# Opening and output projection of a hybrid decoder step: the norm_g spread ahead, masks late on VectorE, banks of their own for the projection, and last stores on two queues

## The chip, the cores and the metric

The kernel runs on one core of a Trainium2 chip. The metric is device microseconds (us) of one execution. The kernel before takes 1124.75 us, the median of 3 runs (1123.86 to 1125.27). Engines are named as in the profile: TensorE is PE (its weight load PEld), VectorE is DVE, ScalarE is ACT, GpSimd is POOL, SyncE is SP.

## What is computed

One decoder layer and a final RMSNorm serve 256 prompt tokens and 64 sample tokens (8 sequences of 8), so 320 tokens of width 2048, all in float32:

```
h = rms_norm(x, norm_g);  p = h @ w_in                    # 2048 -> 12416 columns
y_a = RWKV-7 recurrence of columns of p, times a SiLU gate   # 16 heads of 64
y_b = HGRN2 recurrence of columns of p, times a SiLU gate    # 8 heads of 128
merged = sigmoid(ga) * (y_a @ proj_a) + sigmoid(gb) * (y_b @ proj_b)
y = rms_norm(x + merged @ w_out, final_norm_g)
```

The new states of both recurrences and the last projected row are outputs too.

## The kernel before

Every float32 product is made of three float32r matmuls: both operands are split into a high part (a cast) and a low part (what the cast lost), and hi·hi, lo·hi and hi·lo are summed in one PSUM bank. A block of weights is 1024 rows by 128 columns, 512 KB; ScalarE casts its high part and a second engine subtracts for the low part.

**The opening** (lines 375 to 673) ends with the first tile of the input projection, whose order on TensorE, ScalarE, VectorE and GpSimd is written out by hand. norm_g comes as four rows of 512 (`gq`); ScalarE and VectorE split it into `gr` (lines 574 and 575), four matmuls with selector matrices `sel` spread it over 128 partitions (`gps`, line 578), and VectorE copies it out to `gb` (line 579). Ahead of that VectorE fills the constants `yz`, `qz`, `rs_a`, `rs_b` and others, and behind it `arp`. `warm(n)` issues n matmuls on ones that feed nothing. For each of three token tiles, `squares` and `scale` (ScalarE) find 1/rms, `gain` (VectorE) multiplies by it and by `gb`, `turn` (TensorE) transposes, `high` (ScalarE) and `low` (VectorE) split the transposed tile into `hhi` and `hlo`. `first(part, k4)` is twelve groups of four matmuls of the first projected tile. `half` splits half a weight block, `divide` a whole one, both with GpSimd subtracting (lines 619 and 402). There are three block buffers; `fetch(b, c0, k8)` loads a block into buffer b from SP's queue, and so waits until the block there before it has been split. Loads of small rows (line 420) go through the same queue.

GpSimd also builds masks ahead of `half`: `mk[:, 2]`, two products at line 474, and `mu8`, four casts at line 494 of `mf`.

Next come `rows` and the old shift state, transposed on TensorE and copied by VectorE to `cols` (line 660) and `sst` (line 664).

**The middle** is recorded and put in an order by a planner; every instruction of it carries line 1448. Its order on each engine is fixed ahead of time. It begins with `wd_ad` and `bounds`: VectorE takes `neg` and the first `lbt` difference from `cols`, ScalarE takes an exponential of `lbt`, VectorE goes on with it, and ScalarE and VectorE split the next weight blocks and make `uQ`, `lora_a`, `wst` and `ast`. The first matmul of the middle that needs these is `a<-lora_a,ast`.

**The merge** (lines 1476 to 1494) holds two banks `psf` for `ppa` and `ppb`; its last VectorE reader of a bank is line 1488. **The output projection** (from line 1506) takes six banks from a pool `pso`: three per column block of 512, in two generations, one bank for each token tile. Its matmuls are lines 1531 to 1537, `add` adds the residual and squares on ScalarE. The last column block goes tile by tile, and the third tile (64 rows) in two halves of 256 columns. Each tile then gets its 1/rms (lines 1591 to 1593), four quarter products (lines 1596 to 1600) and two stores from SP's queue (lines 1598 and 1601).

Of the kernel before, what the change touches and what calls it, by code (L numbers as in the profile page):

```python
# [294 lines left out]
def hybrid_step(ctx, tc, x_prompt, x_sample, state_rwkv, state_hgrn, state_shift, norm_g, w_in,  # L295
# [19 lines left out]
    def ctile(shape, name, dt=F32, pool=rconst):  # L315
        return pool.tile(shape, dt, name=name, tag=name)
# [59 lines left out]
    with tc.tile_pool(name="start", bufs=1) as st, \  # L376
# [27 lines left out]

        for k8 in range(2):
            fetch(k8, 128 * 24, k8)

        gr = st.tile([64, 512], F32R, name="gr")
        sel = st.tile([64, 4, 128], F32R, name="sel")
# [13 lines left out]
        for r0, t_ in ((W0, w0), (A0, a0), (KK_, k_k), (KA, k_a), (LW, ln_w), (LB, ln_b), (LG, lb_logits)):  # L423
# [3 lines left out]
        ssr = st.tile([100, 2, 128], F32, name="ssr")  # L427
        nc.sync.dma_start(ssr, state_shift[0].rearrange("s (r c) -> (s r) c", c=128)
                          .rearrange("(j q) c -> q j c", j=2))
        fetch(2, 0, 0)  # L430


        id64 = ctile([128, 64], "id64")
        G.tensor_add(id64, ident[:, 0:64], ident[:, 64:128])
# [37 lines left out]
        blk = seqm[:, :, None].to_broadcast([128, 8, 8])  # L472
        for x in range(2):
            G.tensor_mul(mk[:, 2, x].rearrange("p (s i) -> p s i", i=8),
                         mk[:, 0, x].rearrange("p (s i) -> p s i", i=8), blk)


        mf = st.tile([32, 3, 32], F32, name="mf")
# [2 lines left out]
        for n, sz in enumerate((8, 8, 16)):  # L481
# [8 lines left out]
            G.memset(lv[:, :, 0, :], 0.0)  # L490
            keep_ge(lv[:, :, 1, :], [[-2 * sz, nb], [0, sz]], 0, 1)
            keep_ge(lv[:, :, 1, :], [[2 * sz, nb], [0, sz]], sz - 1, -1)
        for g in range(4):
            G.tensor_copy(mu8[32 * g:32 * g + 32], mf)

        junk = st.tile([128, D], F32, name="junk")
        ssq = [st.tile([128, 2], F32, name=f"ssq{j}") for j in range(3)]

# [40 lines left out]
        def warm(n):  # L539
            for _ in range(n):  # L540
                T.matmul(wps[:, :256], ones[:, :128], ones, start=True, stop=True)

        tps = {}
        with tc.manual_schedule(engines={mybir.EngineType.PE, mybir.EngineType.Activation, mybir.EngineType.DVE,
# [10 lines left out]
                    V.memset(t_[sl, sl].bitcast(F32), x)  # L555
            V.tensor_sub(jr_cent, ident, jr_mean.bitcast(F32))

            yz = ctile([128, 2, 2, 2, 64], "yz")
            yd = ctile([128, 2, 2, 64], "yd")
            qz = ctile([128, NSEQ, 32], "qz")  # L560
# [9 lines left out]
            V.memset(rs_a[:, NP_::8], 0.0)  # L570
            V.memset(rs_b, 1.0)
            V.memset(rs_b[:, ::8], 0.0)

            S.copy(gr[0:4], gq)
            V.tensor_sub(gr[32:36], gq, gr[0:4].bitcast(F32))
            for c_ in range(4):
                ps = pst.tile([128, 512], F32, name="gps", tag="t")
                T.matmul(ps, sel[:, c_], gr, start=True, stop=True)
                V.tensor_copy(gb[:, 512 * c_:512 * c_ + 512], ps)
            V.memset(arp, 0.0)  # L580
            warm(16)
            squares(2)
            scale(2)
            gain(2, 0, 2)
# [70 lines left out]
            first(1, 2)  # L655
            first(2, 2)
            divide(2, 1, G)
            ps = pst.tile([128, 512], F32, name="cps", tag="t")
            T.transpose(ps[:, :128], rows, ident)
            V.tensor_copy(cols, ps[:, :106])  # L660
# [795 lines left out]

    ms = fin.tile([128, KT, 2, NS], F32R, name="ms")

    prj = ExitStack()
    fpr = prj.enter_context(tc.tile_pool(name="fpr", bufs=1))  # L1460
    psf = prj.enter_context(tc.tile_pool(name="psf", bufs=2, space=PSUM))
# [41 lines left out]


    last = ctx.enter_context(tc.tile_pool(name="last", bufs=1))
    pso = ctx.enter_context(tc.tile_pool(name="pso", bufs=2, space=PSUM))
    ssq = last.tile([128, 3, 5], F32, name="ssq")
    rs = [last.tile([128, 1], F32, name=f"rs{j}") for j in range(3)]

# [29 lines left out]
    def add(pt, j, n, c0, w=512):  # L1539
        y = yx[j][:, c0:c0 + w]  # L1540
        if j < 2:
            V.tensor_add(y, y, pt[:, :w])
        else:
            for sl in HS:
                V.tensor_add(y, y, pt[sl, :w])
        jk = last.tile([128, 512], F32, name="jk", tag="jk")
        m = y.shape[0]
        S.activation(jk[:m, :w], y, AF.Square, accum_out=ssq[:m, j, n:n + 1])

    out_tiles = lambda: [pso.tile([128, 512], F32, name=f"po{j}", tag=f"o{j}") for j in range(3)]  # L1550
    tail, coming = [], []
    with tc.manual_schedule(engines={mybir.EngineType.PE}):
        for n in range(3):
            pts = out_tiles()
            for kk in range(8):
                hi, lo = columns(n, kk)
                for q in range(2):
                    for j in range(3):
                        rows(pts[j], j, 2 * kk + q, hi[:, q], lo[:, q])
                step = 8 * n + kk  # L1560
                if step in (1, 2, 3):
                    j = step - 1
                    nc.sync.dma_start(yx[j], x_prompt[0, 128 * j:128 * j + 128, :] if j < 2 else
                                      x_sample.rearrange("b l d -> (b l) d"))
                if step == 4:
                    nc.sync.dma_start(fg, final_g[None, :].to_broadcast([128, D]))
                if step % 2 == 0 and 6 <= step < 20:
                    coming.append(fetch_columns(3, len(coming), last, "t", 2))
                if step % 2 == 1 and 9 <= step < 23:
                    t_ = len(tail)  # L1570
                    tail.append(divide_columns(coming[t_], last, str(t_)))
            for j in range(3):
                add(pts[j], j, n, 512 * n)
                y = yx[j][:, 512 * n:512 * n + 512]
                V.tensor_mul(y, y, fg[:y.shape[0], 512 * n:512 * n + 512])

    with tc.manual_schedule(engines={mybir.EngineType.PE, mybir.EngineType.Activation, mybir.EngineType.DVE}):
        tail.append(columns(3, 7))
        pts = out_tiles()
        for j in range(3):  # L1580

            w = 512 if j < 2 else 256
            for n, pt in enumerate((pts[j],) if j < 2 else (pts[j], pso.tile([128, 512], F32, name="po0", tag="o0"))):
                cs = slice(w * n, w * n + w)
                for k in range(KT):
                    hi, lo = tail[k // 2]
                    rows(pt, j, k, hi[:, k % 2, cs], lo[:, k % 2, cs])
                add(pt, j, 3 + n, 1536 + w * n, w)
            m = yx[j].shape[0]
            r = rs[j][:m]  # L1590
# [4 lines left out]
            y = [yx[j][:, 512 * n:512 * n + 512] for n in range(4)]  # L1595
            V.tensor_scalar(y[0], y[0], r, 0.0, op0=ALU.mult, op1=ALU.add)
            S.activation(y[1], y[1], AF.Copy, scale=r)
            nc.sync.dma_start(dst[:, :1024], yx[j][:, :1024])
            V.scalar_tensor_tensor(y[3], y[3], r, fg[:m, 1536:], op0=ALU.mult, op1=ALU.mult)
            S.activation(y[2], y[2], AF.Copy, scale=r)  # L1600
            nc.sync.dma_start(dst[:, 1024:], yx[j][:, 1024:])


# [26 lines left out]
```

## Time and profile before

| | |
|---|---|
| runs, median of 3 | 1124.75 us |
| the profiled execution | 1124.7 us |
| its span, first to last instruction | 1122.0 us |
| PE busy | 1102.9 us, 98% of the span |
| DVE / ACT / POOL busy | 760.4 / 693.2 / 192.8 us |
| chain that ended last | PE 94%, POOL 2%, ACT 2%, issue 1% |

The profiled execution is 2.7 us longer than its span, which starts with the first instruction. An engine is idle for most of its time without harm where another sets the pace; here TensorE does from about 29 us to 1114 us of the span, and what it waits for there and what lies ahead of it and behind it is what a change can save.

### The profile page before, as it was taken

Reading aid. Unit: us, or ns where it says so; the run is one execution under the profiler, and the core shown is the slowest. Engines: PE = TensorE matmul, PEld = TensorE weight load, DVE = VectorE, ACT = ScalarE, POOL = GpSimd, SP = SyncE. Lnnn points to the kernel's source line nnn. Section 1 sums busy time; section 2 is a strip of 40 time slices with the busy share of each in tenths; the row PEclk is TensorE's granted clock in tenths of the full one; section 3 lists DMA queues with packets and bytes.
Section 4 is the critical chain, followed back from the end, with each engine's and each line's share of the span. In section 5 each row is a group of like instructions: output and inputs, shape, how many; then the busy total and the mean of one; then the engine's idle time right before and its main releaser. Section 6 shows DMA issues by size and latency. Waiting matters only on the chain.

```text
span 1122.0 us, 23659 instructions
## 1 busy us (share of the span) xinstructions
PE 1102.9 (98%) x9240; PEld 1066.5 (95%) x9240; DVE 760.4 (68%) x1618; ACT 693.2 (62%) x1572; POOL 192.8 (17%) x411
## 2 busy tenths in 40 slices
PE   6999999999999999999999999999999999999997
PEld 5999999999999999999999999999999999988886
DVE  8778888887887887887887876444444444437532
ACT  6777777677778678677776876444444444436322
POOL 9531231221311411412312200000000000000000
PEclk9999999999999999999999999999999999999999
DMA  6743545435435436435444354555555555587512
GB/s 177 202 130 107 152 118 146 136 100 157 125 96 158 131 105 165 133 106 159 117 132 137 101 142 142 147 151 150 149 151 150 150 150 149 151 256 267 173 35 93
DMA packets 283107, 159.87 MB, mean 142 GB/s; under 512 B 22893, under 2 KB 273264, under 8 KB 282356
## 3 DMA queue, kind: packets, MB, share of 16 engines
q1 hardware_dynamic: 282996, 158.37, 49.5%
q8 instruction: 72, 1.18, 0.5%
q14 instruction: 39, 0.32, 0.1%
HBM read 148.53 MB, written 9.81 MB: 141 GB/s over the span
## 4 chain that ended last, share of the span: by engine, by line
PE 94%; POOL 2%; ACT 2%; issue 1%; DVE 0%; DMA 0%; ACTq 0%; POOLq 0%; DVEq 0%
PE mps L1448 41%; PE a L1448 10%; PE mps L359 6%; PE mps L360 6%; PE mps L361 6%; PE b L1448 3%; PE po L1531 3%; PE po L1533 3%; PE po L1532 3%; PE ppa L359 2%; PE ppb L360 2%; PE ppb L359 2%; PE ppa L360 2%; PE ppb L361 2%; PE ppa L361 2%; PE y L1448 1%
## 5 line engine op out<-in xcount | busy, mean ns | idle before, releaser
L1448 PE MATMUL mps<-hhi,whi 128*128 128x320 f32 x1088 | 345.1, 317 | 0.0
L1448 PE MATMUL mps<-hlo,whi 128*128 128x320 f32 x1088 | 344.6, 317 | 0.0
L1448 PE MATMUL mps<-hhi,wlo 128*128 128x320 f32 x1088 | 344.1, 316 | 0.0
L1448 PEld LDWEIGHTS mps<-hhi,whi 128*128 128x128 f32 x1088 | 205.0, 188 | 3.6 <-issue 2.7
L1448 PEld LDWEIGHTS mps<-hlo,whi 128*128 128x128 f32 x1088 | 205.1, 188 | 1.1 <-issue 0.4
L1448 PEld LDWEIGHTS mps<-hhi,wlo 128*128 128x128 f32 x1088 | 205.0, 188 | 0.7
L349 ACT CAST whi<-raw 128x1024 fp32r<-128x1024 f32 x88 | 92.4, 1050 | 162.7 <-PE mps L360 107.3
L350 DVE TENSOR_TENSOR wlo<-raw,whi 128x1024 fp32r<-128x1024 f32 x88 | 107.8, 1226 | 124.9 <-ACT whi L349 124.8
L1448 DVE TENSOR_TENSOR wlo<-raw,whi 128x1024 fp32r<-128x1024 f32 x134 | 164.7, 1229 | 17.1 <-ACT whi L1448 15.9
L1448 ACT CAST whi<-raw 128x1024 fp32r<-128x1024 f32 x134 | 140.2, 1046 | 57.0 <-PE mps L1448 54.6
L361 PE MATMUL mps<-hhi,wlo 128*128 128x320 f32 x448 | 138.7, 310 | 0.0
L359 PE MATMUL mps<-hhi,whi 128*128 128x320 f32 x448 | 138.7, 310 | 0.0
L360 PE MATMUL mps<-hlo,whi 128*128 128x320 f32 x448 | 138.7, 309 | 0.0
L361 PEld LDWEIGHTS mps<-hhi,wlo 128*128 128x128 f32 x448 | 84.1, 188 | 0.0
L360 PEld LDWEIGHTS mps<-hlo,whi 128*128 128x128 f32 x448 | 84.1, 188 | 0.0
L359 PEld LDWEIGHTS mps<-hhi,whi 128*128 128x128 f32 x448 | 84.1, 188 | 0.0
L1520 DVE TENSOR_TENSOR wlo<-raw,whi 128x1024 fp32r<-128x1024 f32 x32 | 38.6, 1223 | 39.0 <-ACT whi L1519 38.9
L1519 ACT CAST whi<-raw 128x1024 fp32r<-128x1024 f32 x32 | 33.0, 1050 | 48.5 <-DMA raw<-in_w_out_dram 21.3
L1448 POOL TENSOR_TENSOR vm<-v,seq 96x512 fp32r<-96x512 f32 x16 | 16.9, 1054 | 200.1 <-ACT uK L1448 152.4
L1531 PE MATMUL po<-whi,mhi 128*128 128x512 f32 x128 | 50.1, 392 | 0.7 <-DVE gbt L1488 0.7
L1533 PE MATMUL po<-wlo,mhi 128*128 128x512 f32 x128 | 50.1, 391 | 0.0
L1532 PE MATMUL po<-whi,mlo 128*128 128x512 f32 x128 | 50.0, 391 | 0.0
(435 smaller groups left out, 2244.0 us busy)
## 6 DMA issues: line engine op xcount, KB each, us to landing
raw<-in_w_in_dram SPq DMA_DIRECT2D x194, 512.0 KB
raw<-in_w_out_dram SPq DMA_DIRECT2D x32, 512.0 KB
raw<-in_proj_a_dram SPq DMA_DIRECT2D x16, 512.0 KB
raw<-in_proj_b_dram SPq DMA_DIRECT2D x16, 512.0 KB
s<-in_state_hgrn_dram SPq DMA_DIRECT2D x8, 512.0 KB
out_dram<-s SPq DMA_DIRECT2D x8, 512.0 KB
s<-in_state_rwkv_dram SPq DMA_DIRECT2D x8, 256.0 KB
out_dram<-s SPq DMA_DIRECT2D x8, 256.0 KB
```

Of the source, the lines that this page charges most:

```text
L349: S.copy(hi[:, ks], raw[:, ks])
L350: sub.tensor_sub(lo[:, ks], raw[:, ks], hi[:, ks].bitcast(F32))
L359: T.matmul(dst, hi[:, q, :], xhi[:, k, :], start=(k == 0), stop=False)
L360: T.matmul(dst, hi[:, q, :], xlo[:, k, :], start=False, stop=False)
L361: T.matmul(dst, lo[:, q, :], xhi[:, k, :], start=False, stop=(k == nk - 1))
L1448: o.fn(*o.args, **o.kw)
L1519: S.copy(hi, raw)
L1520: V.tensor_sub(lo, raw, hi.bitcast(F32))
L1531: T.matmul(pt, h, hi, start=first, stop=False)
L1532: T.matmul(pt, l, hi, start=False, stop=False)
L1533: T.matmul(pt, h, lo, start=False, stop=end)
```

## The change

- The split and spreading of norm_g moves ahead of the constants; its four copies out of PSUM alternate between ScalarE and VectorE; `warm(16)` becomes `warm(20)`.
- The load of the third weight block is issued ahead of the small rows.
- The products for `mk[:, 2]` and the casts for `mu8` move from GpSimd to VectorE, behind the split of the third block.
- The output projection takes its first generation of banks from a pool opened ahead of `psf` (`pso[0]`), the second behind it (`pso[1]`).
- At the end, the squares carry the factor 1/D, the sum of the earlier partial squares and the epsilon are made ahead of the last `add`, and the logarithm takes that sum as its bias and the last partial as its input. The third tile's columns 1536 to 1791 get final_norm_g during the last matmuls. The products are cut anew, and the store of columns 1024 to 2047 goes first, from SP's queue, that of columns 0 to 1023 second, from ScalarE's queue.

```diff
+        fetch(2, 0, 0)                                   # ahead of the rows, line 404
...
-        fetch(2, 0, 0)                                   # behind ssr, line 430
...
-        for x in range(2):
-            G.tensor_mul(mk[:, 2, x]..., mk[:, 0, x]..., blk)
...
-        for g in range(4):
-            G.tensor_copy(mu8[32 * g:32 * g + 32], mf)
...
             V.tensor_sub(jr_cent, ident, jr_mean.bitcast(F32))
+            S.copy(gr[0:4], gq)
+            V.tensor_sub(gr[32:36], gq, gr[0:4].bitcast(F32))
+            for c_ in range(4):
+                ps = pst.tile([128, 512], F32, name="gps", tag="t")
+                T.matmul(ps, sel[:, c_], gr, start=True, stop=True)
+                (V.tensor_copy if c_ % 2 else S.copy)(gb[:, 512 * c_:512 * c_ + 512], ps)
             ... (constants)
-            S.copy(gr[0:4], gq)
-            ... (the same with V.tensor_copy alone)
             V.memset(arp, 0.0)
-            warm(16)
+            warm(20)
...
             divide(2, 1, G)
+            for x in range(2):
+                V.tensor_mul(mk[:, 2, x]..., mk[:, 0, x]..., blk)
+            for g in range(4):
+                V.tensor_copy(mu8[32 * g:32 * g + 32], mf)
             ps = pst.tile([128, 512], F32, name="cps", tag="t")
...
+    pso = [ctx.enter_context(tc.tile_pool(name="pso0", bufs=1, space=PSUM))]
     prj = ExitStack()
...
-    pso = ctx.enter_context(tc.tile_pool(name="pso", bufs=2, space=PSUM))
+    pso.append(ctx.enter_context(tc.tile_pool(name="pso1", bufs=1, space=PSUM)))
...
-        S.activation(jk[:m, :w], y, AF.Square, accum_out=ssq[:m, j, n:n + 1])
+        S.activation(jk[:m, :w], y, AF.Square, scale=D ** -0.5, accum_out=ssq[:m, j, n:n + 1])
...
+                if 512 == w * (n + 1):
+                    V.tensor_reduce(r, ssq[:m, j, :3 + n], axis=mybir.AxisListType.X, op=ALU.add)
+                    V.tensor_add(r, r, eps_n[:m])
                 add(pt, j, 3 + n, 1536 + w * n, w)
+                if j == 2 and n == 0:
+                    y = yx[j][:, 1536:c1]
+                    V.tensor_mul(y, y, fg[:m, 1536:c1])
-            V.tensor_reduce(r, ssq[:m, j, :4 + j // 2], axis=mybir.AxisListType.X, op=ALU.add)
-            S.activation(r, r, AF.Ln, scale=1.0 / D, bias=eps_n[:m])
+            S.activation(r, ssq[:m, j, 2 + 512 // w:3 + 512 // w], AF.Ln, bias=r)
             S.activation(r, r, AF.Exp, scale=-0.5)
+            V.scalar_tensor_tensor(y[:, c1:], y[:, c1:], r, fg[:m, c1:], op0=ALU.mult, op1=ALU.mult)
+            S.activation(y[:, 0:512], y[:, 0:512], AF.Copy, scale=r)
+            V.tensor_scalar(y[:, 1024:c1], y[:, 1024:c1], r, 0.0, op0=ALU.mult, op1=ALU.add)
+            nc.sync.dma_start(dst[:, 1024:], y[:, 1024:])
+            S.activation(y[:, 512:768], y[:, 512:768], AF.Copy, scale=r)
+            V.tensor_scalar(y[:, 768:1024], y[:, 768:1024], r, 0.0, op0=ALU.mult, op1=ALU.add)
+            nc.scalar.dma_start(dst[:, :1024], y[:, :1024])
```

Here c1 is 1536 for the first two tiles and 1792 for the third.

## Rows read from the trace of the kernel before

**Rows 1.** TensorE's waits over the span: total us, times, longest us.
```profile
PE gps L578 <- DVE gr L575: 6.8, 1, 6.8
PE a L1448 <- DVE ast L1448: 0.9, 1, 0.9
...
PE po L1531 <- DVE gbt L1488: 0.7, 1, 0.7
PE mps L612 <- POOL wlo L619: 0.4, 1, 0.4
```

**Rows 2.** Chain that ended last, 0 to 60 us: start, us, what.
```profile
28.56 4.51 DMA raw<-in_w_in_dram
...
33.17 1.05 ACT whi L1448
...
38.12 0.53 PE a L1448 x2
```

**Rows 3.** Timeline of the opening, until 12.5 us: start, us, engine, line, operation, count.
```profile
3.26 0.48 DVE L563 MEMSET yz<- 128x512 f32 x1
...
5.93 0.68 DVE L575 TENSOR_TENSOR gr<-gq,gr 4x512 fp32r<-4x512 f32 x1
6.64 1.91 ACT L502 ACTIVATE junk<-xt 64x2048 f32<-64x2048 f32 x1 [3.54 <-DMA xt<-in_x_sample_dram]
...
6.76 2.04 PE L578 MATMUL gps<-gr,sel 64*128 64x512 f32 x4 [6.76 <-DVE gr L575]
...
7.56 2.49 DVE L579 COPY gb<-gps 128x512 f32<-128x512 f32 x4 [0.95 <-PE gps L578]
...
8.73 3.78 PE L541 MATMUL wps<-ones 128*128 128x256 f32 x16
...
10.26 1.12 DVE L580 MEMSET arp<- 128x1280 f32 x1 [0.21 <-issue]
...
11.30 6.19 DVE L513 SCALAR_TENSOR_TENSOR xt<-xt,ssq,gb 64x1024 f32<-64x1024 f32 x6
```

**Rows 4.** The same timeline, GpSimd alone, until 29 us.
```profile
10.02 6.27 POOL L474 TENSOR_TENSOR mk<-mk,seqm 128x64 f32<-128x64 f32 x2
...
21.14 5.04 POOL L619 TENSOR_TENSOR wlo<-raw,whi 128x512 fp32r<-128x512 f32 x4
...
26.12 2.41 POOL L402 TENSOR_TENSOR wlo<-raw,whi 128x1024 fp32r<-128x1024 f32 x1
```

**Rows 5.** The same timeline, ScalarE and VectorE, 24 to 31 us.
```profile
24.77 1.06 ACT L401 CAST whi<-raw 128x1024 fp32r<-128x1024 f32 x1
...
27.29 0.27 DVE L660 COPY cols<-cps 128x106 f32<-128x106 f32 x1 [1.57 <-PE cps L659]
...
27.75 0.82 DVE L1448 TENSOR_SCALAR neg<-cols 128x16 f32<-128x16 f32 x1
...
30.53 0.21 ACT L1448 ACTIVATE lbt<-lbt 128x8 f32<-128x8 f32 x1
```

**Rows 6.** Timeline of the end, from 1115 us.
```profile
1115.49 0.15 DVE L1591 TENSOR_REDUCE rs<-ssq 64x1 f32<-64x5 f32 x1 [0.64 <-ACT jk L1548]
1115.67 0.29 ACT L1592 ACTIVATE rs<-rs,eps_n 64x1 f32<-64x1 f32 x1 [0.22 <-DVE rs L1591]
...
1116.24 0.48 DVE L1596 TENSOR_SCALAR xb<-xb,rs 64x512 f32<-64x512 f32 x1 [0.60 <-ACT rs L1593]
1116.64 0.74 DVE L1599 SCALAR_TENSOR_TENSOR xb<-xb,rs 64x512 f32<-64x512 f32 x1
...
1116.98 0.49 SPq L1598 DMA_DIRECT2D out_dram<-xb  x1
1117.60 0.51 SPq L1601 DMA_DIRECT2D out_dram<-xb  x1
```

**Rows 7.** Busy time by stretch: us, engines (count), granted clock, DMA share, GB/s.
```profile
1110.00:1112.80 2.80, 2.80 (x26) 2.80 (x25) 0.83 (x2) 0.51 (x2) 0.00 (x0) 1.00 0.94 375
1118.10:1120.80 2.70, 0.00 (x0) 0.00 (x0) 0.00 (x0) 0.00 (x0) 0.00 (x0) 0.60 0.92 194
```

More of the change, by code (lines that the diff above doesn't have):

```diff
@@ L471, in hybrid_step @@
                 keep_ge(mk[sl, c_], [[1, 2], [1, 64]], -1, -1)
-        blk = seqm[:, :, None].to_broadcast([128, 8, 8])
-        for x in range(2):
-            G.tensor_mul(mk[:, 2, x].rearrange("p (s i) -> p s i", i=8),
-                         mk[:, 0, x].rearrange("p (s i) -> p s i", i=8), blk)
         mf = st.tile([32, 3, 32], F32, name="mf")
@@ L572, in hybrid_step @@
             V.memset(rs_b[:, ::8], 0.0)
-            S.copy(gr[0:4], gq)
[L575 to L579, printed above, removed]
             V.memset(arp, 0.0)
-            warm(16)
+            warm(20)
             squares(2)
@@ L657, in hybrid_step @@
             divide(2, 1, G)
+            blk = seqm[:, :, None].to_broadcast([128, 8, 8])
+            for x in range(2):
+                V.tensor_mul(mk[:, 2, x].rearrange("p (s i) -> p s i", i=8),
+                             mk[:, 0, x].rearrange("p (s i) -> p s i", i=8), blk)
+            for g in range(4):
+                V.tensor_copy(mu8[32 * g:32 * g + 32], mf)
             ps = pst.tile([128, 512], F32, name="cps", tag="t")
@@ L1547, in add @@
         m = y.shape[0]
-        S.activation(jk[:m, :w], y, AF.Square, accum_out=ssq[:m, j, n:n + 1])
-    out_tiles = lambda: [pso.tile([128, 512], F32, name=f"po{j}", tag=f"o{j}") for j in range(3)]
+        S.activation(jk[:m, :w], y, AF.Square, scale=D ** -0.5, accum_out=ssq[:m, j, n:n + 1])
+    out_tiles = lambda n: [pso[n % 2].tile([128, 512], F32, name=f"po{j}", tag=f"o{j}") for j in range(3)]
     tail, coming = [], []
@@ L1553, in hybrid_step @@
         for n in range(3):
-            pts = out_tiles()
+            pts = out_tiles(n)
             for kk in range(8):
@@ L1578, in hybrid_step @@
         tail.append(columns(3, 7))
-        pts = out_tiles()
+        pts = out_tiles(3)
         for j in range(3):
             w = 512 if j < 2 else 256
-            for n, pt in enumerate((pts[j],) if j < 2 else (pts[j], pso.tile([128, 512], F32, name="po0", tag="o0"))):
+            m = yx[j].shape[0]
+            r = rs[j][:m]
+            c1 = D - w
+            for n, pt in enumerate((pts[j],) if j < 2 else (pts[j], pso[0].tile([128, 512], F32, name="po0", tag="o0"))):
                 cs = slice(w * n, w * n + w)
@@ L1587, in hybrid_step @@
                     rows(pt, j, k, hi[:, k % 2, cs], lo[:, k % 2, cs])
+                if 512 == w * (n + 1):
+                    V.tensor_reduce(r, ssq[:m, j, :3 + n], axis=mybir.AxisListType.X, op=ALU.add)
+                    V.tensor_add(r, r, eps_n[:m])
                 add(pt, j, 3 + n, 1536 + w * n, w)
-            m = yx[j].shape[0]
-            r = rs[j][:m]
-            V.tensor_reduce(r, ssq[:m, j, :4 + j // 2], axis=mybir.AxisListType.X, op=ALU.add)
-            S.activation(r, r, AF.Ln, scale=1.0 / D, bias=eps_n[:m])
+                if j == 2 and n == 0:
+                    y = yx[j][:, 1536:c1]
+                    V.tensor_mul(y, y, fg[:m, 1536:c1])
+            S.activation(r, ssq[:m, j, 2 + 512 // w:3 + 512 // w], AF.Ln, bias=r)
             S.activation(r, r, AF.Exp, scale=-0.5)
             dst = y_prompt[0, 128 * j:128 * j + 128, :] if j < 2 else y_sample.rearrange("b l d -> (b l) d")
[L1595 to L1601, printed above, removed]
+            y = yx[j]
+            V.scalar_tensor_tensor(y[:, c1:], y[:, c1:], r, fg[:m, c1:], op0=ALU.mult, op1=ALU.mult)
[5 more added lines that the diff above has]
+            nc.scalar.dma_start(dst[:, :1024], y[:, :1024])
 _INS = ['x_prompt', 'x_sample', 'state_rwkv', 'state_hgrn', 'state_shift', 'norm_g', 'w_in',
```

## The prediction

> **What bounds the kernel.** I read the chain that ended last first: 94% of it is TensorE, so only the ends of the span and TensorE's waits can give time. TensorE's waits come next [rows 1]: the first matmul stands 6.8 us until norm_g is split, then 0.4 us for GpSimd's low weights, 0.9 us for `ast`, and 0.7 us at the first matmul of the output projection. Then the chain of the opening [rows 2]: the load that ends at 33.07 holds ScalarE's cast at 33.17, and that leads to the matmul `a` at 38.12. Last the timelines of the opening, engine by engine [rows 3 to 5], and of the end [rows 6]. The reader should see that VectorE is late with norm_g for no reason but its place in line, and that GpSimd begins on the weights only at 21.14 because masks lie ahead of them.
>
> **The spread of norm_g.** VectorE could take the subtraction at 3.26 instead of 5.93 [rows 3]. The first of the four matmuls began 0.83 us behind it (6.76 against 5.93) and they took 2.04, so they run from 4.09 to 6.13. VectorE needed 2.49 for four copies; its two now end about 0.7 behind the last matmul, at 6.8, and ScalarE's two about 6.3, inside the 3.54 us in which ScalarE waits for the samples until 6.64. The constants then take what they took, 2.67 (3.26 to 5.93), and `arp` 1.04 (10.26 to 11.30): the gains begin at 6.8 + 3.7 = 10.5 instead of 11.30, 0.8 us earlier. Most of the possible 2.7 us stays with VectorE, since the constants only change places with norm_g. Four more warm matmuls at 3.78/16 = 0.24 are 0.95 us: they end at 6.06 + 4.7 = 10.8, while the first transpose must wait for the first gain, about 1.2 us from 10.5. They cost nothing; without that cover they would cost at most 0.95.
>
> **The load ahead of the small rows.** The block's cast at 24.77 had no wait before it [rows 5], so nothing is gained there. The rows move behind one more 512 KB load; a load behind a full queue took about 4.5 us [rows 2], which puts their landing near 20 us, ahead of `cols` at 27. Cost 0; without that slack at most those 4.5 us.
>
> **The masks leave GpSimd.** The two products at 10.02 took 6.27 us [rows 4]. Without them and the casts GpSimd can start on the weights when ScalarE's first cast is there, near 17 instead of 21.14, so TensorE's 0.4 us wait goes. By then TensorE is 0.8 + 0.4 = 1.2 us ahead. ScalarE follows TensorE there, so the cast of the third block ends at 25.83 - 1.2 = 24.65, GpSimd subtracts from 24.65 to 27.05 instead of 26.12 to 28.53, and the load behind it lands 1.5 us earlier. Since both TensorE's head start and this load are 1.2 to 1.5 us ahead and 0.9 us of waiting at `a` lies between, the opening could give 1.5 to 2.0 us.
>
> **The masks arrive on VectorE.** They are two products of 64 columns and four casts of 96; by `cols`, 0.27 us for 106 columns [rows 5], I take 0.2 us each, 1.2 in all. VectorE waited 1.57 us ahead of `cols`, which seems to hide them. But rows of both engines show that each can hold the other up. `neg`, 16 columns, took 0.82 us and ended at 28.57, just when GpSimd's subtraction ended at 28.53 [rows 4, 5]. And the two mask products took GpSimd 6.27 us while the gains ran. In the changed kernel the gains of the second half meet GpSimd's first subtractions (5.04/4 = 1.26 us each, from about 17 on), which delays VectorE by up to 0.9 us. So the first mask product becomes ready about when, or just after, the long subtraction starts at 24.65, and waits until 27.05. Two products until 27.45; then GpSimd's next subtraction, whose block now is there in time, until 29.85; beside it the casts and `cols`; then `neg`, and the `lbt` difference, some 0.35 us; ScalarE's exponential of `lbt` at 30.2 instead of 30.53 [rows 5]. Everything behind it on ScalarE (two weight casts, `uQ`, `lora_a`, `ast`) keeps its distance, so `a` comes at 37.8 instead of 38.12. TensorE, there 1.2 us earlier, waits 1.75 us instead of 0.85. The opening gives 0.3 us. The bounds: 2.0 us gained if the two engines never meet, and 0.9 us lost if GpSimd does both subtractions in a row (24.65 to 29.45) before VectorE gets one product: then 1.2 for the masks, 0.46 for `cols` and `sst`, 0.35 for `neg` and `lbt` put the exponential at 31.45. I take 0.3 gained, between them, because `neg` shows one instruction's wait and not two.
>
> The Trainium skill has the rule for it ("SBUF — State Buffer", section "Who interferes with whom"): a VectorE instruction with two SBUF inputs, or in a two-port mode, and a GpSimd instruction that reads SBUF shut each other out, and "issue order, not op shape, decides who blocks". The 0.82 us of `neg` agrees. By it the opening gives about 1.8 us if the product is issued before the subtraction and 0.3 if behind it; which of them comes first is too close for the rows to tell.
>
> **The banks.** TensorE's 0.7 us at the first matmul of the output projection ends when VectorE has read the last bank of the merge (line 1488) [rows 1]. With the first generation in other banks that reason is gone; the next thing it needs, the first weights and the first merged rows, is long there, since ScalarE and VectorE work one to three blocks ahead. I take the whole 0.7 us; the bounds are 0, if another wait replaces it, and 0.7.
>
> **The end.** The logarithm can begin where the reduction began, 1115.49 instead of 1115.67 [rows 6]: 0.18 us. Then VectorE has the 256-column product (0.74 for 512, so about 0.45) and the 768-column one (0.48 for 512, about 0.6): from 1116.06 they end near 1117.1, and the first store goes out at 1117.1 instead of 1116.98. The second goes out near 1117.4 instead of 1117.60. The two stores of 64 rows moved 194 GB/s between them from 1118.10 to 1120.80, while those of 128 rows reached 375 [rows 7]: with 64 rows it is the transfer that is slow, and the second store had no gap to lose. So what counts is when the first goes out: 0.1 us lost. If the two queues ran side by side at full rate, the second's own time would count, about 0.9 us gained; if ScalarE's queue, which carries no store before, is slower to start than SP's, up to 0.6 lost.
>
> The Trainium skill speaks against the second queue ("DMA: Bandwidth & Descriptors", section "Issuing engines are not separate DMA queues"): transfers started by different engines run on the same 16 DMA engines and interleave. By it this part is the 0.1 us lost; no run here shows it yet.
>
> **The sum.** -0.3 - 0.7 + 0.1 = -0.9 us on the profiled execution's 1124.7: 1123.8 us. The median of the runs is 0.05 higher, which changes nothing.
>
> **The rivals.**
> - *VectorE gets its products in first.* For it: VectorE's 1.57 us of room. Against it: `neg`. Opening -1.8, sum -1.8 - 0.7 + 0.1 = -2.4: 1122.3 us; with stores side by side as well 1121.4.
> - *GpSimd does both subtractions first.* For it: the second now needs no load that is late. Opening +0.9, sum +0.3: 1125.0 us.
> - *TensorE's clock falls at `a`* (slower). In the case before, TensorE would arrive at 36.1 and wait until 39.0, about 3 us. The granted clock of 0.60 from 1118.10 to 1120.80 [rows 7], with only 1.0 and 0.5 to mix, puts its fall at about 1118.6, 4.7 us after the last matmul; the 0.9 us waits cost none. If a wait of some 4 us at `a` brings the level of 1.2 GHz for 4 us, half of these are lost, 2 us: sum +2.3, 1127.0 us. [...]
> - *The banks don't help*, since another wait stands at the same place: sum -0.2, 1124.5 us.
>
> **Chances and range.** Forecast 0.44, VectorE first 0.28, GpSimd first 0.16, banks 0.06, clock 0.06. About 0.2% (2.25 us) is what can be told from no change. The first rival lies on that line or beyond, so faster gets 0.27; slower by as much needs the clock or a slow queue on top of a loss, 0.06; the same 0.67. The range runs from 1121.6, nearly all of the first rival, to 1125.6, past the second; the forecast's own is 1123.2 to 1124.4.
>
> **What would show it.** In the new profile: gains from about 10.5; no wait for GpSimd's low weights; the first mask product on VectorE far longer than 0.2 us, ending with a GpSimd subtraction; ScalarE's `lbt` exponential near 30.2, and a wait at `a` of more than 0.9 us. No wait at line 1531's first matmul. The last store issued near 1117.4 less what the front gave, and the stores' rate still near 200 GB/s. If `lbt` comes before 29, the two engines did not meet and the prediction is too slow; if gains don't start before 11, its first step is wrong.

## The result and the profile after

Before: 1124.36 us (median of 22 runs, 1123.65 to 1125.27). After: 1126.03 us (22 runs, 1124.15 to 1128.46); ratio 1.0013 [1.0007, 1.0018]. The change makes the kernel slightly slower. The profiled execution took 1126.66 us with a span of 1124.9, against 1124.7 and 1122.0. The spans differ by 2.9 us, the times by 2.0: what lies around the span was 2.7 us in the run profiled before and 1.76 in this one, and it is about 1.7 in most runs of both. So the working below goes by the spans. It is the working of one execution, and one of the longer ones: the 22 spans of the changed kernel reach from 1122.4 to 1126.7 us, with a median of 1124.0.

TensorE runs the same list of matmuls in both kernels, so the first question is how late one and the same matmul starts in each. The table gives its start less its start before, worked out from the two traces (+ is later); the rows below the second are the experiments.

| kernel (start before, us) | first of block 0 (18.22) | `cols` transpose (26.98) | `a` (38.12) | 57.26 | 988.34 | 1025.77, output projection | last (1113.67) |
|---|---|---|---|---|---|---|---|
| after | +1.36 | +0.68 | +2.30 | +3.69 | +3.72 | +2.81 | +2.81 |
| e1 masks back | +1.53 | +0.84 | -0.01 | -0.01 | -0.08 | -0.99 | -0.99 |
| e2 spread back | -0.13 | +0.02 | +1.33 | +2.90 | +2.93 | +2.02 | +2.02 |
| e3 warm 28 | -0.28 | -0.15 | +1.17 | +2.74 | +2.72 | +1.81 | +1.81 |
| e4 banks and end | -0.09 | +0.23 | -0.14 | -0.15 | -0.14 | -1.05 | -0.49 |
| e5 e1, warm 28 | -0.24 | -0.26 | -0.77 | -0.76 | -0.79 | -1.70 | -0.95 |
| e6 products early | +1.62 | +0.93 | +2.19 | +3.74 | +3.74 | +3.11 | +3.21 |
| e7 gains first | -1.37 | -2.05 | -2.56 | -2.57 | -2.57 | -3.47 | -3.47 |
| e8 one queue | +0.92 | +0.61 | -0.34 | -0.35 | -0.31 | -1.21 | -1.21 |
| e9 casts on ScalarE | +1.97 | +1.30 | +0.44 | +0.44 | +0.39 | -0.52 | -0.52 |
| e10 products last | -1.38 | -1.92 | -1.92 | -1.92 | -1.97 | -2.88 | -2.88 |
| e11 last block on VectorE | -1.35 | -1.86 | -2.36 | -2.36 | -2.33 | -3.24 | -3.24 |

All of the loss is made by 44 us, and nothing is added in the 940 us after it. The banks give 0.91 back at one place. Then 1124.9 - 2.81 = 1122.1 against 1122.0: the end costs 0.1.

TensorE's waits of after (total us, times, longest), which answer to [rows 1]:

```profile
PE gps L554 <- DVE gr L551: 4.4, 1, 4.4
PE a L1446 <- DVE ast L1446: 2.5, 1, 2.5
PE tps L517 <- DVE xt L505: 2.0, 1, 2.0
```

The waits for GpSimd's weights and for the bank at the output projection are gone. In their place the wait at `a` grew from 0.9 to 2.5 us, and one of 2.0 us stands ahead of the first transpose. In the kernel before, that transpose follows the warm matmuls (done at 12.51) without a wait; its own wait for a gain, 0.8 us, came only at 16.89:

```profile
12.51 0.79 PE L525 MATMUL tps<-ident,xt 64*128 64x64 f32 x8
```

The timeline of the opening, answering to [rows 3]:

```profile
3.24 1.05 DVE L551 TENSOR_TENSOR gr<-gq,gr 4x512 fp32r<-4x512 f32 x1
4.44 2.04 PE L554 MATMUL gps<-gr,sel 64*128 64x512 f32 x4 [4.44 <-DVE gr L551]
6.42 3.94 PE L533 MATMUL wps<-ones 128*128 128x256 f32 x20
6.52 0.69 DVE L555 COPY gb<-gps 128x512 f32<-128x512 f32 x1 [0.16 <-PE gps L554]
7.27 0.48 DVE L562 MEMSET yz<- 128x512 f32 x1
...
10.11 1.12 DVE L572 MEMSET arp<- 128x1280 f32 x1 [0.19 <-issue]
11.15 6.06 DVE L505 SCALAR_TENSOR_TENSOR xt<-xt,ssq,gb 64x1024 f32<-64x1024 f32 x6
12.36 0.85 PE L517 MATMUL tps<-ident,xt 64*128 64x64 f32 x8 [2.01 <-DVE xt L505]
```

The warm matmuls moved 2.3 us ahead with norm_g, the gains only 0.15. The twenty took 3.94 us, and not the 4.7 that the spacing of before would make: they started 0.21 us apart until 9.36 and 0.12 apart from there on, where the trace's record of the granted clock begins, at 1.00. In the kernel before it begins at 12.74, and all sixteen stood at the wider spacing. So TensorE, done at 10.35, stood idle for 2.01 us. The windows of after show what followed, there and behind the wait at `a`. A line gives the length of the stretch, the busy time (and count) of PE, PEld, DVE, ACT and POOL, the granted clock (1.00 or 0.50), the DMA share and GB/s:

```profile
9.40:12.70 3.30, 1.29 (x13) 1.09 (x13) 3.00 (x5) 3.22 (x5) 3.19 (x3) 1.00 1.09 342
12.80:19.50 6.70, 6.70 (x36) 6.09 (x34) 5.71 (x7) 3.60 (x9) 6.23 (x10) 0.50 0.67 163
19.70:40.00 20.30, 17.57 (x123) 17.04 (x122) 18.64 (x33) 13.95 (x31) 13.18 (x20) 1.00 0.57 151
40.10:43.40 3.30, 2.98 (x11) 3.01 (x12) 2.33 (x6) 2.41 (x5) 2.63 (x9) 0.50 1.20 290
```

The same two stretches that stand at 0.50 here, in the kernel before:

```profile
12.80:19.50 6.70, 5.84 (x47) 4.62 (x45) 6.70 (x9) 4.75 (x11) 6.55 (x14) 1.00 0.59 158
40.10:43.40 3.30, 3.30 (x26) 3.30 (x25) 2.38 (x5) 2.97 (x9) 1.83 (x8) 1.00 0.56 137
```

TensorE ran at 1.2 GHz instead of 2.4 in both: 36 matmuls instead of 47, and 11 instead of 26. The second stretch is the step from +2.30 to +3.69 in the table, 1.39 us. What made `a` late is in the timeline of 26 to 41 us, answering to [rows 4, 5]:

```profile
26.59 4.79 POOL L402 TENSOR_TENSOR wlo<-raw,whi 128x1024 fp32r<-128x1024 f32 x2 [1.23 <-ACT whi L401]
26.71 4.75 DVE L652 TENSOR_TENSOR mk<-mk,seqm 128x64 f32<-128x64 f32 x2
31.38 0.84 DVE L655 CAST mu<-mf 32x96 uint8<-32x96 f32 x4
32.25 0.27 DVE L658 COPY cols<-cps 128x106 f32<-128x106 f32 x1
32.37 0.38 ACT L1446 COPY pad<-mps 128x256 f32<-128x256 f32 x1 [3.55 <-issue]
32.71 0.17 DVE L1446 TENSOR_SCALAR neg<-cols 128x16 f32<-128x16 f32 x1
32.98 0.21 ACT L1446 ACTIVATE lbt<-lbt 128x8 f32<-128x8 f32 x1 [0.23 <-DVE lbt L1446]
...
40.42 0.60 PE L1446 MATMUL a<-lora_a,ast 128*128 128x320 f32 x1 [2.46 <-DVE ast L1446]
```

Two products of 64 columns took VectorE 4.75 us, just as long as GpSimd's two subtractions of 1024 beside them. `cols` is 5 us later than in [rows 5], ScalarE's exponential of `lbt` 2.45, and `a` 2.30. The late VectorE reached ScalarE in two ways. ScalarE stood idle for 3.55 us ahead of `pad`, the first of its instructions in the middle, and went on 0.15 us behind VectorE's last cast, which ended at 32.22; SP's next load was issued at 32.36. The profile names no reason for that wait; it fits memory of the opening that is free only when `mf` has been read. The wait for `lbt` itself added 0.23 us.

The end of after, answering to [rows 6, 7]:

```profile
1118.87 0.48 DVE L1603 SCALAR_TENSOR_TENSOR xb<-xb,rs 64x256 f32<-64x256 f32 x1 [1.20 <-ACT rs L1600]
1119.27 0.61 DVE L1605 TENSOR_SCALAR xb<-xb,rs 64x768 f32<-64x768 f32 x1
1119.90 0.49 SPq L1606 DMA_DIRECT2D out_dram<-xb  x1
1120.22 0.54 ACTq L1609 DMA_DIRECT2D out_dram<-xb  x1
```

And the window in which these two stores move:

```profile
1120.80:1123.00 2.20, 0.00 (x0) 0.00 (x0) 0.00 (x0) 0.00 (x0) 0.00 (x0) 0.50 0.92 194
```

Less the 2.81 us by which all of it is late, the first store goes out 0.11 later than before, the second 0.19 earlier, and the rate is the same 194 GB/s.

### The profile page after: what moved, and what is told of

Read it like the earlier page. It is cut to its first block, busy times and chain, and to the rows that moved or that the text cites. A ratio compares the mean times of both kernels' runs of the same rounds, so it can differ in the third digit from the quotient of the medians.

```text
span 1124.9 us, 23677 instructions
## 1 busy us (share of the span) xinstructions
PE 1106.3 (98%) x9244; PEld 1070.6 (95%) x9244; DVE 766.5 (68%) x1629; ACT 694.1 (62%) x1574; POOL 190.3 (17%) x405
## 4 chain that ended last, share of the span: by engine, by line
PE 96%; ACT 2%; DVE 1%; issue 1%; POOL 0%; DVEq 0%; ACTq 0%; POOLq 0%
PE mps L1446 42%; PE a L1446 10%; PE mps L361 6%; PE mps L359 6%; PE mps L360 6%; PE b L1446 3%; PE po L1533 3%; PE po L1531 3%; PE po L1532 3%; PE ppb L361 2%; PE ppb L359 2%; PE ppa L361 2%; PE ppa L359 2%; PE ppb L360 2%; PE ppa L360 2%; PE y L1446 1%
```

## The experiments

**The theory** was that two parts of the change lose time, each in its own way: the masks hold VectorE behind GpSimd's subtractions, which makes `a` late and drops the clock behind its wait; and the spread leaves TensorE idle ahead of the first transpose, which drops the clock there. **Rivals**: one of the two is the cause of everything, or late memory or loads are. The median of the kernel before lies between 1123.9 and 1124.0 us beside these runs, and the ratios are taken against its runs.

**e1, masks back on GpSimd**, all else of the change kept.

```diff
+            G.tensor_mul(mk[:, 2, x].rearrange("p (s i) -> p s i", i=8),
...
+            G.tensor_copy(mu8[32 * g:32 * g + 32], mf)
...
             divide(2, 1, G)
-                V.tensor_mul(mk[:, 2, x].rearrange("p (s i) -> p s i", i=8),
...
-                V.tensor_copy(mu8[32 * g:32 * g + 32], mf)
```

> The changed kernel with the masks back on GpSimd, where the kernel before has them. Theory: the masks on VectorE carry the loss at `a`. Then VectorE's `cols` comes back from 32.25 to about 27.3 to 28, ScalarE's `lbt` exponential to 30 to 31, `a` from 40.42 to about 38.1, and the granted clock does not fall at 40. The fall at 12.77 stays, since TensorE still idles from its last warm matmul to the first transpose, but the wait at `a` takes up what it costs: opening about 0, banks and end -0.8, so about 1123.6 us against 1124.4. Rival: the slow TensorE of 12.77 to 19.60 is what makes everything late; then `a` stays above 39.5 and the time near 1125.5 to 1126.

Measured: 1122.65 us, ratio 0.9987 [0.9979, 0.9996]; the span is 0.8 us shorter than before, as expected, and the median 1.3. `cols` at 28.13, the exponential at 30.40, `a` at 38.11 without any wait. The matmul `a` and two windows of it:

```profile
38.11 0.39 PE L1446 MATMUL a<-lora_a,ast 128*128 128x320 f32 x1
12.60:19.30 6.70, 6.70 (x38) 6.24 (x37) 5.93 (x7) 3.15 (x8) 6.51 (x14) 0.50 0.64 156
40.10:43.40 3.30, 3.30 (x26) 3.30 (x24) 2.12 (x3) 3.10 (x8) 2.09 (x9) 1.00 0.61 151
```

The clock still falls at the first transpose, and not at `a`. So without the masks the loss is gone: 3.7 us by the two traces, 2.9 by the medians, each against the kernel before. The loads stand here as in the change, so they are not its cause. Without the masks the change is faster than the kernel before.

**e2, norm_g spread where it was**, with 16 warm matmuls; masks on VectorE.

```diff
-            S.copy(gr[0:4], gq)
...
-                (V.tensor_copy if c_ % 2 else S.copy)(gb[:, 512 * c_:512 * c_ + 512], ps)
...
             V.memset(rs_b[:, ::8], 0.0)
+            S.copy(gr[0:4], gq)
...
+                V.tensor_copy(gb[:, 512 * c_:512 * c_ + 512], ps)
             V.memset(arp, 0.0)
-            warm(20)
+            warm(16)
```

> The changed kernel with norm_g spread where the kernel before has it (16 warm matmuls); masks still on VectorE. Theory: the gap ahead of the first transpose falls back to 0.8 us, so the clock does not fall at 12.77; the masks still hold VectorE until a GpSimd subtraction ends, twice, so `cols` comes near 31 to 32 and `a` near 39.5 to 40.4, the wait at `a` is 2.5 to 3.2 us and the clock falls there again: +2.5 to +3.7 in the opening, -0.8 behind it, 1126 to 1127 us. Rival: the products were late only because the slow TensorE shifted them against the subtractions; then `cols` comes by 29, `a` by 38.1, and the time is 1123.6 or less.

Measured: 1127.09 us, 1.0026 [1.0016, 1.0036], 0.1 above what was expected; the profiled run, 1125.87, is the shortest of its nine. TensorE's wait at `a` is 2.2 us, 0.3 below the expected range. VectorE's products, and then two windows:

```profile
26.79 3.71 DVE L651 TENSOR_TENSOR mk<-mk,seqm 128x64 f32<-128x64 f32 x2
```

```profile
12.80:19.50 6.70, 5.95 (x47) 4.71 (x45) 6.70 (x9) 4.85 (x12) 6.70 (x11) 1.00 0.65 157
40.40:43.60 3.20, 3.20 (x15) 3.16 (x14) 1.95 (x4) 3.01 (x7) 2.93 (x13) 0.50 0.87 208
```

No fall at the first transpose, but the masks wait all the same and the clock falls behind `a`: the second fall needs no first. What the first one costs the changed kernel is less clear. In the traces e2 is 0.8 us ahead of the change, but by the medians it is slower (1127.09 against 1126.03, and 1124.3 against 1124.0 by the spans), so a loss by the early spread is not shown in the usual execution.

**e3, 28 warm matmuls instead of 20**, all else as in the change.

```diff
-            warm(20)
+            warm(28)
```

> The changed kernel with 28 warm matmuls in place of 20, so that TensorE has work until about 12.3 us, when the first gain ends. Theory: the idle 2.0 us before the first transpose are what let the clock fall at 12.77; bridged, the clock stays at 2.4 GHz there, transposes run at the spacing of before and the first matmul of part 0 begins near 18.2 instead of 19.57. The masks still hold VectorE, so `a` stays near 40 with a wait of 3 us or more and the fall at 40: time about that of the changed kernel, 1125.5 to 1126.5 us. Rival: the first fall is what made the masks late as well; then `a` comes by 38.5 and the time is 1123.6 to 1124.4. Second rival: the fall at 12.77 has another cause and comes again.

Measured: 1125.61 us, 1.0009 [1.0000, 1.0018]. The 28 were done at 11.34 and not at 12.3, since they too ran 0.12 us apart from 9.4 on; but the wait ahead of the first transpose is 1.0 us instead of 2.0, and the fall is gone (a clock of 1.00 in the first window). `a` still waits 2.2 us:

```profile
12.36 0.71 PE L517 MATMUL tps<-ident,xt 64*128 64x64 f32 x8 [1.02 <-DVE xt L505]
12.80:19.50 6.70, 5.64 (x44) 4.39 (x42) 6.70 (x9) 5.34 (x12) 6.70 (x9) 1.00 0.67 161
40.20:43.50 3.30, 3.30 (x15) 3.26 (x14) 1.98 (x4) 3.10 (x8) 2.95 (x13) 0.50 0.83 199
```

Only the warm matmuls, and with them the idle time, were changed, so idleness in the opening was the cause of the first fall. Of the eleven runs, five have spans of 1122.3 to 1122.4 and six of 1123.9 to 1124.9. A gap of 1.5 us is what the fall behind `a` costs here (+1.17 to +2.74 in the table), so it may come in some executions only; just one run has a trace, so this is argued and not shown. The runs of the change itself fit: in six the mean granted clock is 0.996 or 0.997, with spans of 1122.4 to 1123.4, and in sixteen, the profiled one among them, 0.993 or 0.994, with 1123.6 to 1126.7.

**e4, banks and end alone**, opening of the kernel before.

```diff
+    pso = [ctx.enter_context(tc.tile_pool(name="pso0", bufs=1, space=PSUM))]
...
+    pso.append(ctx.enter_context(tc.tile_pool(name="pso1", bufs=1, space=PSUM)))
...
+            nc.scalar.dma_start(dst[:, :1024], y[:, :1024])
```

> The kernel before with only the banks and the end of the change; its opening untouched. Theory: all of the loss is made before 44 us; between 44 and 996 us the changed kernel's TensorE stands 3.69 to 3.73 us late without a step, then the banks give back 0.91, and the last stores land 0.12 later against TensorE's end. So -0.9 + 0.1 = -0.8 us: 1123.6 us against 1124.4. Rival: the end costs or gives more than the one profile shows (two queues that start the stores apart), from -1.8 to 0.

Measured: 1123.14 us, 0.9991 [0.9982, 1.0000], the -0.8 that was expected. In its profiled run the banks give 0.91 as well, and 0.56 is lost again between 1032 and 1040 us, where TensorE waits 0.3 us for VectorE's low weights; e5 loses 0.75 in the same place, e6 0.1, the others nothing. What sets that stays open.

**e5, e1 with 28 warm matmuls.**

```diff
-            warm(20)
+            warm(28)
```

> The changed kernel with the masks back on GpSimd and 28 warm matmuls. With 20 the clock still fell at 12.52, TensorE ran 0.84 us late to `cols`, and yet `a` came at 38.11, without a wait. Theory: the fall at the first transpose costs nothing there, since `a` follows ScalarE's and VectorE's chain to `ast`. Bridged, the clock stays up, TensorE is some 1 us earlier, waits that long at `a`, and `a` comes at 37.7 to 38.2; time within 0.4 us of 1122.65. Rival: the chain to `ast` follows TensorE (through the transposes that ScalarE and VectorE read), and `a` comes 0.8 us or more earlier: 1121.8 us or less.

Measured: 1122.72 us, 0.9987 [0.9978, 0.9996]: the time is that of e1. Its trace speaks for the rival: `a` comes 0.76 us earlier than in e1, so the chain to `ast` does follow TensorE; what was won is lost in the output projection, as told at e4. But e8 below has the opening of e1, with the same fall, and its `a` is only 0.43 us behind that of e5. So the first fall is worth 0.4 to 0.8 us at `a` where nothing else holds `a`, and nothing that shows in the time.

**e6, the two products ahead of the gains on VectorE**, the casts of `mu8` left late.

```diff
             V.memset(arp, 0.0)
+            blk = seqm[:, :, None].to_broadcast([128, 8, 8])
+            for x in range(2):
+                V.tensor_mul(mk[:, 2, x].rearrange("p (s i) -> p s i", i=8),
...
             warm(20)
...
             divide(2, 1, G)
-            blk = seqm[:, :, None].to_broadcast([128, 8, 8])
-            for x in range(2):
-                V.tensor_mul(mk[:, 2, x].rearrange("p (s i) -> p s i", i=8),
...
```

> The changed kernel with the two mask products on VectorE moved ahead of the gains, right behind the memset of `arp`; the four casts of `mu8` stay late on VectorE. Theory: not the work but its place beside GpSimd's long subtractions cost the time. Near 11.2 GpSimd runs only short instructions, so the products take 0.2 us each (at most 0.5), the gains begin near 11.6, the casts take 0.84 us in all near 26.7, `cols` comes near 27.6, `lbt` by 31, `a` near 38.1 to 38.5, and the clock does not fall at 40: 1122.7 to 1123.4 us. Rival: the six instructions cost VectorE their time wherever they stand, or the casts' release of the opening's memory alone makes `a` late; then `a` is past 39.3 and the time 1125 or more.

Measured: 1125.53 us, 1.0012 [1.0003, 1.0021]. This expectation failed:

```profile
11.15 0.30 DVE L575 TENSOR_TENSOR mk<-mk,seqm 128x64 f32<-128x64 f32 x2
...
26.84 4.78 POOL L402 TENSOR_TENSOR wlo<-raw,whi 128x1024 fp32r<-128x1024 f32 x2 [1.23 <-ACT whi L401]
26.98 5.13 DVE L655 CAST mu<-mf 32x96 uint8<-32x96 f32 x4
32.15 0.27 DVE L658 COPY cols<-cps 128x106 f32<-128x106 f32 x1
```

Early, both products take 0.30 us. But now the first two casts stand where the products stood and take 2.33 and 2.36 us, one GpSimd subtraction each; the last two take 0.20 each. The theory missed that a cast from SBUF waits like a product. What remained open was whether this, or the late reading of `mf`, which keeps the opening's memory, makes `a` late.

**e9, e6 with the casts on ScalarE.**

```diff
             divide(2, 1, G)
-            for g in range(4):
-                V.tensor_copy(mu8[32 * g:32 * g + 32], mf)
...
+            for g in range(4):
+                S.copy(mu8[32 * g:32 * g + 32], mf)
             for j in range(4):
                 S.copy(seq4[32 * j:32 * j + 32], seqm[0:32, 0:4])
```

> The run with the products ahead of the gains, and with the four casts of `mu8` on ScalarE, ahead of its copies of `seq4`; nothing of the masks is left on VectorE behind GpSimd's long subtractions. In the run before it the first cast took 2.33 us and the second 2.36, each until a GpSimd subtraction ended (29.25, 31.62), and the other two 0.20 each. Theory: this lock carries the loss, and not that `mf` is read late, which keeps the opening's memory. Then `cols` comes near 27.9, the four casts cost ScalarE 0.8 us (near 27.6 to 28.4) that it has idle, `a` comes at 38.0 to 38.6, the clock does not fall at 40, and the time is 1122.6 to 1123.4 us. Rival: the late reader of `mf` is what holds ScalarE, SP and GpSimd; it still reads at 28.4, some 2.5 us later than without, and `a` stays past 39.3, the time 1124.5 or more.

Measured: 1122.74 us, 0.9988 [0.9979, 0.9997]. The casts, still late, cost ScalarE 1.11 us, and VectorE is free:

```profile
27.96 1.11 ACT L667 CAST mu<-mf 32x96 uint8<-32x96 f32 x4
28.59 0.27 DVE L656 COPY cols<-cps 128x106 f32<-128x106 f32 x1 [1.18 <-PE cps L655]
30.60 0.37 ACT L1446 COPY pad<-mps 128x256 f32<-128x256 f32 x1
```

`a` comes at 38.57 without a wait, and the clock does not fall there; at the first transpose it does, behind a wait of 2.4 us. So the loss comes from VectorE's waits behind GpSimd, and reading `mf` until 29.07 costs nothing. But its memory is not cleared as a link: in after `mf` is read until 32.22 and in e6 until 32.11, and in both `pad` began some 0.15 us later. Whether VectorE's late casts held ScalarE by the memory or by `lbt`, which came 0.2 us behind, no run tells apart. The four casts may even be late, if not on VectorE.

**e8, both stores of e1 from SP's queue.**

```diff
-            nc.scalar.dma_start(dst[:, :1024], y[:, :1024])
+            nc.sync.dma_start(dst[:, :1024], y[:, :1024])
```

> The changed kernel with the masks back on GpSimd, and with both stores of a row block issued by SP. Theory: the two queues give nothing by themselves, since the two stores share the rate of the first run (194 GB/s between them): the last landing stands within 0.15 us of where it stands with two queues, measured from TensorE's last matmul, and the time is that of the run with two queues, 1122.65, to 0.3 us. Rival: SP issues the second store 0.5 us or more later, behind the first one's issue, and the end is as much longer.

Measured: 1122.85 us, 0.9986 [0.9977, 0.9995]. From the last matmul's place, the span ends at 1120.9 + 1.21 = 1122.1, and in e1 at 1121.2 + 0.99 = 1122.2: one queue or two makes no difference, though SP issues the second store at 1116.47, 0.59 behind the first, and ScalarE in e1 0.32 behind.

**e7, gains first**: e1 with `rs_b` behind the second gain and `arp` in the late place where the masks had been.

```diff
-            V.memset(rs_b, 1.0)
-            V.memset(rs_b[:, ::8], 0.0)
-            V.memset(arp, 0.0)
             warm(20)
...
             gain(2, 2, 2)
+            V.memset(rs_b, 1.0)
+            V.memset(rs_b[:, ::8], 0.0)
...
             divide(2, 1, G)
+            V.memset(arp, 0.0)
```

> The changed kernel with the masks back on GpSimd, and with the constants `rs_b` behind the second gain and `arp` late, where the changed kernel has the masks, so that the gains of the samples need not wait for them. Theory: spreading norm_g ahead gave only 0.15 us because the constants stand between it and the gains. Now the gains begin near 9.7 instead of 11.15, the first transpose near 10.9, 0.5 us behind the last warm matmul, and the clock does not fall at 12.5; GpSimd, held up by the gains, is free some 0.7 to 1.5 us earlier. The chain to `ast` moves with it in part: `a` near 37.0 to 37.8, time 1121.6 to 1122.4 us. Rival: the loads set the opening and nothing is gained over 1122.65; second rival: the late `arp` holds VectorE ahead of `cols`, and `a` comes at 38.5 or later.

Measured: 1120.50 us, 0.9970 [0.9958, 0.9981], the fastest of all, 1.1 us below the lower end of what the theory expected. Its timeline:

```profile
9.35 2.51 DVE L511 SCALAR_TENSOR_TENSOR xt<-xt,ssq,gb 64x1024 f32<-64x1024 f32 x2
10.68 0.71 PE L523 MATMUL tps<-ident,xt 64*128 64x64 f32 x8
...
10.87 1.40 POOL L473 TENSOR_TENSOR mk<-mk,seqm 128x64 f32<-128x64 f32 x2
...
23.87 2.42 POOL L402 TENSOR_TENSOR wlo<-raw,whi 128x1024 fp32r<-128x1024 f32 x1
24.68 1.12 DVE L655 MEMSET arp<- 128x1280 f32 x1 [0.22 <-issue]
26.11 0.21 DVE L1446 TENSOR_SCALAR neg<-cols 128x16 f32<-128x16 f32 x1
26.46 2.42 POOL L402 TENSOR_TENSOR wlo<-raw,whi 128x1024 fp32r<-128x1024 f32 x1 [0.17 <-ACT whi L401]
35.56 0.38 PE L1446 MATMUL a<-lora_a,ast 128*128 128x320 f32 x1 [0.35 <-DVE ast L1446]
```

This is what the spread was for: gains 1.95 us earlier than in [rows 3], no wait ahead of the first transpose and at most 0.8 us behind it, GpSimd's products 1.40 us instead of 6.27 [rows 4], and `a` 2.56 earlier. `arp`, written by VectorE without reading SBUF, is not held beside the subtraction. `neg` ends in the 0.17 us between two subtractions.

**e10, e7 with the products last on GpSimd.**

```diff
                 keep_ge(mk[sl, c_], [[1, 2], [1, 64]], -1, -1)
-            G.tensor_mul(mk[:, 2, x].rearrange("p (s i) -> p s i", i=8),
...
             divide(0, 1, G)
+                G.tensor_mul(mk[:, 2, x].rearrange("p (s i) -> p s i", i=8),
```

> The run with the gains first, and with the two mask products behind all weight subtractions on GpSimd (their first reader comes past 60 us). Theory: GpSimd then reaches the weights some 1.2 to 1.4 us earlier (17.83 in the run before it), the load behind them is issued up to 1.5 us earlier than at 21.45, and `a`, at 35.56 there, comes 0.3 to 1 us earlier: 1119.5 to 1120.2 us against 1120.5. Rival: GpSimd is no longer what the opening waits for, and the time is the same to 0.3 us. Second rival: the late products meet VectorE's subtractions behind 29 us and hold up the middle's first instructions on GpSimd: `a` later, 1121 or more.

Measured: 1121.06 us, 0.9976 [0.9967, 0.9985], slower than e7, so the theory failed; the second rival has the time, but the products on GpSimd held up nothing (0.32 and 0.29 us, from 28.58). GpSimd was early as hoped and the load behind it was issued at 20.22 instead of 21.45. That closed the gap between the two long subtractions, and `neg` was shut out, 2.07 us for 16 columns:

```profile
23.84 4.78 POOL L402 TENSOR_TENSOR wlo<-raw,whi 128x1024 fp32r<-128x1024 f32 x2 [0.70 <-ACT whi L401]
26.59 2.07 DVE L1446 TENSOR_SCALAR neg<-cols 128x16 f32<-128x16 f32 x1
...
36.20 0.39 PE L1446 MATMUL a<-lora_a,ast 128*128 128x320 f32 x1 [0.84 <-DVE ast L1446]
```

**e11, e10 with the last block's subtraction on VectorE.**

```diff
-            divide(0, 1, G)
+            divide(0, 1, V)
```

> The run with the products last, and with the subtraction of the last block (1024 columns) on VectorE instead of GpSimd. In that run the earlier load made GpSimd's two long subtractions follow each other (23.84 to 28.62), and VectorE's `neg`, 16 columns, took 2.07 us until the second one ended, so the `lbt` exponential came at 28.76 and `a` at 36.20, later than the 35.56 with the products early, where `neg` got in between the two. Theory: the same lock again, at another instruction. With one subtraction left on GpSimd, VectorE's takes 1.23 us after `sst`, from about 26.6 to 27.8, `neg` takes 0.2, the exponential comes near 28.1 to 28.3 and `a` near 35.3 to 35.8: 1120.2 to 1120.7 us against 1121.06. Rival: `neg` was only covering another wait (the load of `w2a`, issued at 26.95), and `a` stays at 36.1 or later: 1121 us.

Measured: 1120.74 us, 0.9970 [0.9960, 0.9981]. `neg` is short again and `a` at 35.76:

```profile
26.64 1.24 DVE L402 TENSOR_TENSOR wlo<-raw,whi 128x1024 fp32r<-128x1024 f32 x1
27.80 0.20 DVE L1446 TENSOR_SCALAR neg<-cols 128x16 f32<-128x16 f32 x1
```

The lock explains `neg` too. `a` moved by 0.44 us, the last matmul by 0.36 and the median by 0.32, to just above what was expected. e7 stays ahead by 0.24 us in the median and by 0.1 in the spans.

## Why the prediction was wrong

It gave 1123.8 us, with 1121.6 to 1125.6 as its range; the median was 1126.03. Its sum was -0.9 (-0.3 opening, -0.7 banks, +0.1 end); the spans show +3.7, -0.9, +0.1.

- **"The gains begin at ... 10.5"**: wrong, 11.15. The subtraction of norm_g took 1.05 us instead of 0.68 and the matmuls began 1.20 behind it instead of 0.83, so VectorE's last copy ended at 7.2 instead of 6.8; the constants up to the gains took 3.88 instead of 3.71. It is a sum of small sizes, but it left 0.15 of the 0.8 us. The working had named the reason itself, that the constants only change places with norm_g; e7 shows what moving them gives.
- **"They cost nothing"**, the warm matmuls: the prediction compared their end (10.8) with the first gain's end (11.7) and saw cover, with a gap of 0.9. They ended at 10.35, since from 9.36 they ran 0.12 us apart and the working had 0.24 for all, and the first gain at 12.36. The gap was 2.01 us and the clock fell behind it. TensorE was then 0.7 to 1.4 us late where it was to be 1.2 early. GpSimd's long subtraction came at 26.59 instead of the expected 24.65; in e3, without the fall, at 25.47, so 1.1 of these 1.9 us go with the fall.
- **"The first mask product ... waits until 27.05. Two products until 27.45"**: the failed step. The lock was seen and its place was right, but each of the two products waited for a subtraction of its own (29.09, 31.46). The prediction held one wait for the likeliest, since `neg` shows one; but `neg` is one instruction. With it went the step to `lbt`: 32.98 instead of 30.2. The rival in which GpSimd does both subtractions first has this mechanism, with +0.9 for the opening, since it kept the early start of 24.65 and no clock.
- **`a`**: forecast 37.8 with a wait of 1.75; 40.42 with 2.46. Its distance from the exponential "keeps", 7.44 us for 7.59, but by luck: before, ScalarE waited 1.38 us on the way for a load, and after, both casts ran in a row and it waited 1.49 for VectorE's `uQ`. Behind `a` the clock stood at 0.50 from 40.1 to 43.4, which cost 1.39, where the sum has nothing. The rival with the clock had the sum nearest to the spans (+2.3 against +2.9), but its condition, a wait of some 4 us, was wrong: 2.1 to 2.5 us were followed by the fall in after, e2, e3 and e6. None was after 0.9 in the kernel before, nor after 0.84 in e10.
- **The banks** were right and larger: 0.91 for 0.7 in after, and 0.90 or 0.91 in all experiments but e6 (0.63). The wait row counts from the end of the merge's last matmul; from its start to the first matmul of the projection were 0.98 us before (995.67 to 996.65) and 0.15 after (999.39 to 999.54).
- **The end** was right: 0.1 us lost, 194 GB/s in both kernels, and e8 shows that the second queue is worth nothing. The Trainium skill ("DMA: Bandwidth & Descriptors", section "Issuing engines are not separate DMA queues") says so: transfers from different engines share the same DMA engines. The trace agrees.
- **The load ahead of the small rows** cost nothing that shows: no `cols` transpose waits for its rows.

The Trainium skill's rule on the shared port ("SBUF — State Buffer", section "Who interferes with whom") agrees for each instruction: "Issue order, not op shape, decides who blocks". The first product started 0.12 us behind the subtraction and ended 0.08 behind its end (29.01). The prediction applied the rule once; it had to be applied to every instruction in the line.

## What to carry to other kernels

Before small work is moved to VectorE beside a run of long GpSimd instructions, count the small instructions that read SBUF: here the first two in the line paid up to one whole GpSimd instruction each, so two cost 4.75 us where their work was 0.3. When a step is moved ahead, look at what still stands between it and its user (the constants ahead of the gains), and at what else moves with it: the warm matmuls went ahead by 2.3 us, their cover by 0.15. A wait on TensorE can cost time behind it as well, here 1.4 us behind the 2.46 at `a`, so a delay of the critical chain and the clock have to be added up together.

## What the runs showed of the hardware

- GpSimd and VectorE took turns, one instruction each, while both had work in line: 2.38 and 2.45 us for the products (after), 2.33 and 2.36 for the casts (e6), and the rest at 0.20 once GpSimd's line was empty. The other way round, by its record, one GpSimd instruction on 32 columns stood from 9.89 to 15.96 us in after, most of it beside VectorE's gains from 11.15 on; in e7 it took 0.20. It began ahead of the gains, so what held it is not shown.
- Held were a product of two SBUF tensors, a float-to-uint8 cast and a `TENSOR_SCALAR` of 16 columns. Not held beside a subtraction were a memset (`arp`, 1.12 us in e7) and the copy of `cols` from PSUM (0.20 us in e7).
- The granted clock fell to 1.2 GHz behind 1.7 to 2.4 us of idle TensorE ahead of the first transpose (after, e1, e6, e8, e9), and behind 2.1 to 2.5 us at `a` (after, e2, e3, e6), there at a cost of 1.4 to 1.6 us. It stayed up where the longest such wait was 1.0 us or less (e3, e5, e7, e10, e11).
